# Later keys' activations made one group ahead and kept on chip, V alone for the first groups, and one norm for all gathered tokens

## The chip, the cores and the metric

The kernel runs on one core of one Trainium2 chip. The metric is the device time of one execution in microseconds (us); before takes 4829.66 us, the median of three runs (4826.51 to 4833.37).

## The reference, cut to what matters

The program is one layer on 512 tokens of width 2048: a mixer (mLSTM and forgetting attention), a cross attention, and a PEER feed-forward net, each followed by a layer norm. The change touches only the last of the three:

```python
def peer_ffn(x, w_pq, sub_keys, expert_u, expert_v):
    ...
    idx = jnp.take_along_axis(cand_i, best_pos, -1)
    g = jax.nn.softmax(best_s, -1)
    ...
    def block(args):
        xt, it, gt = args
        u = expert_u[it]
        a = jnp.einsum('tkd,td->tk', u, xt, preferred_element_type=F32)
        hact = jax.nn.gelu(a, approximate=False) * gt
        return jnp.einsum('tk,tkd->td', hact.astype(x.dtype), expert_v[it])
...
x = layer_norm(DN_ALPHA * x + h, ln_w[l, 2], ln_b[l, 2])
```

There are 16384 experts, 128 keys of 128. Each token takes 8 heads x 16 = 128 of them: a dot product with a row of `peer_u`, a gelu, a gate, and a sum of rows of `peer_v`. Everything is float32.

## The kernel before, in words

**Two ways for the tokens.** The 512 tokens stand in four blocks of 128. The first block's 128 tokens and 96 of the last block's, in two parts of 64 and 32, go the *gathered* way: their rows of `peer_u` and `peer_v` are fetched one by one (`gathered`, L906 to L955). The 288 tokens between (NDENSE) go the *dense* way: all 16384 experts are computed for them, and the gate matrix G, which is zero for experts that a token did not choose, picks the right ones.

**The dense way** has three parts, and most of the last 1760 us.

- `stage_a(c)` (L1269) computes for key c (128 experts) the product of `uT[c]` with the tokens: two weight tiles of 128 x 1024, 48 matmuls with 288 columns. Float32 accuracy is had by splitting each operand in a high and a low part: `split` (L132) makes the high part with a cast on ACT (whi, hph: L133) and the low part with a subtraction on DVE (wlo, hpl: L134), and `products` (L197) issues the three products (L201). A gelu on ACT (L1283) takes the result from PSUM to a tile `ga` (three buffers).
- `stage_h(c)` (L1304) multiplies the activation with key c's gates (L1313, DVE) and splits the product (hph on ACT, hpl on DVE). The split pairs have 18 buffers, for nine keys.
- `stage_o(c0, q)` (L1395) is V: for a group of eight keys (c0 to c0 + 7) and a quarter q of the 2048 output columns, four blocks of one weight tile and 24 matmuls each, summed in four PSUM banks (`po`) and then added to `acc` on DVE (L1422).

Weight tiles arrive through two rings, each with three raw buffers and two or three split ones. SP issues their loads (L145), in program order with all other loads of SP, so ACT and DVE can work about five tiles ahead of PE.

**Spilling.** Activations are computed well ahead of V. `ahead` gives for each key how many stage_a come before it: 76 (LOOK) before the first group, then the other 52 spread over the groups, three or four in a group, put behind V's blocks by `fill` (L1459). All but two of the 128 activations (`spilled`) are written to DRAM after their gelu (`gad`, L1285, issued by ACT) and read back by `fetch` (L1290 to L1302; L1299, issued by SP) up to two keys ahead of their stage_h into four buffers `gb`.

**The gate matrix** is built beside the first pass of stage_a, in 72 batches of four tokens (L1225 to L1255): two comparisons on DVE (L1244), four scalings on ACT (L1249), four matmuls (L1250), four copies on ACT (L1253). Every twelve batches, four DMAs on ACT's queue write the result to DRAM (`gd`, L1255). `fetch` reads it back four keys at a time (L1295, SP, two buffers `G`). The read waits for all the writes, since both name the whole of `gd`.

**The gathered way** runs beside all this: POOL fetches rows (L901), DVE makes dot products (L929) and sums (L932), paced by `fill`, 44 of 194 steps (EARLY) in the first pass (the first block is done before). At the end of each of the two parts, the rows' two or four partial sums are folded with matmuls (L950) and copied back by ACT (L951), and the part is normed by itself: two loads of the norm's weights, broadcast to all partitions (L964), statistics (L972), square root (`rstd`, L245), and four passes on DVE (`fin`, L976 to L983).

**The end.** After the last group `turned_out` (L1352) transposes `acc` back to rows, and `last_rows` (L1366) finishes the norm: square root, transpose of five columns of statistics (L1378), a copy (L1380), small matmuls (L1388), one DVE pass (L1390), output (L1393).

A static order of the instructions on each engine is fixed when the kernel is built: the source gives priorities, and a scheduler with its own estimates of durations puts each engine's instructions in a row. Engines run their row strictly in order.

Of the kernel before, what the change touches and what calls it, by code (L numbers as in the profile page):

```python
# [10 lines left out]
F32 = mybir.dt.float32  # L11
# [10 lines left out]
P = 128  # L22
# [23 lines left out]
def build(tc, I, out):  # L46
    nc = tc.nc
    with ExitStack() as ctx:
# [854 lines left out]
            after(i, last())  # L903
            return rows

        def gathered(t, r0, n, i, last, lag):  # L906


            ei, gg = eid[:, i], egg[:, i]
            xacc = gat.tile([P, D], F32, tag="xacc", bufs=1, name=nm("xacc"))  # L910
            for j in range(0, P, n):
                nc.gpsimd.dma_start(xacc[j:j + n], x2d[t, r0:r0 + n].rearrange("p g c -> p (g c)"))
            dots = gat.tile([P, P], F32, tag="dots", bufs=2, name=nm("dots"))
            held = []

            def use():
                s, rows = held.pop(0)
                k = s % n
                if s == n:

                    al = gat.tile([P, 1], F32, tag="al", bufs=1, name=nm("al"))
                    if n < P:
                        nc.vector.memset(al, 0.0)
                    nc.vector.memset(al[:n], ALPHA)
                    nc.scalar.mul(xacc, xacc, al)
                    nc.scalar.activation(dots[:, :n], dots[:, :n], AF.Gelu)
                    nc.vector.tensor_mul(dots[:, :n], dots[:, :n], gg[:, :n])
                if s < n:
                    after(nc.vector.scalar_tensor_tensor(rows, rows, 1.0, xacc, op0=ALU.mult, op1=ALU.mult,  # L929
                                                         accum_out=dots[:, k:k + 1]), last())  # L930
                else:
                    after(nc.vector.scalar_tensor_tensor(xacc, rows, dots[:, k:k + 1], xacc,  # L932
                                                         op0=ALU.mult, op1=ALU.add), last())

            for s in range(2 * n):
                if len(held) == lag:
                    use()
                held.append((s, gather_rows("peer_v" if s >= n else "peer_u", ei, s % n, last)))
                yield True
            while held:  # L940
                use()
            if n < P:
                fold = gat.tile([P, 64], F32, tag="fold", bufs=1, name=nm("fold"))
                nc.vector.tensor_add(fold[:, :n], ident[:, 0:n], ident[:, n:2 * n])
                for j in range(2 * n, P, n):
                    nc.vector.tensor_add(fold[:, :n], fold[:, :n], ident[:, j:j + n])
                for g in range(4):
                    bank = BK["pool"].tile([P, 512], F32, tag="s1", bufs=1, name=nm("fo"))
                    o = xacc[:, g * 512:(g + 1) * 512]
                    nc.tensor.matmul(bank[:n], fold[:, :n], o, start=True, stop=True)  # L950
                    nc.scalar.copy(o[:n], bank[:n])  # L951
            lw = fin_load(gat)
            fin_stats(i, xacc, range(4), n)
            fin(t * P + r0, i, xacc, lw, n)
            yield True  # L955
# [304 lines left out]
        mn = ctx.enter_context(tc.tile_pool(name="main", bufs=1, reuse_waits="tile"))  # L1260
        acc = mn.tile([P, NK, NDENSE], F32, tag="acc", name="acc")

        LOOK = 76
        EARLY = 44
        GA_N = 3
        J = 8
        gas, hs, gates = {}, {}, [None]

        rings[:] = [W, E]  # L1269

        def stage_a(c):

            bank = sm_bank()[:, :NDENSE]
            for kt in range(2):
# [7 lines left out]
            ga = gap.tile([P, NDENSE], F32, tag="ga", bufs=GA_N, name=nm("ga"))  # L1282
            nc.scalar.activation(ga, bank, AF.Gelu)  # L1283
            if c in spilled:
                nc.scalar.dma_start(gad[c], ga)  # L1285
            else:
                gas[c] = ga

        fetched = {}

        def fetch(c):

            if c % 4 == 0:
                gt = mn.tile([P, NDENSE // GB, 4, GB], F32, tag="G", bufs=2, name=nm("G"))
                nc.sync.dma_start(gt, gd[:, :, c:c + 4])  # L1295
                gates[0] = gt
            if c in spilled:
                ga = mn.tile([P, NDENSE], F32, tag="gb", bufs=4, name=nm("gb"))
                nc.sync.dma_start(ga, gad[c])  # L1299
            else:  # L1300
                ga = gas.pop(c)
            fetched[c] = ga, gates[0]  # L1302

        def stage_h(c):  # L1304
            for f in range(c, min(c + 3, NC_)):
                if f in fetched:
                    continue
                if f != c and f not in spilled:
                    break
                fetch(f)  # L1310
            ga, gt = fetched[c]
            gv = ga.rearrange("p (b t) -> p b t", t=GB)
            nc.vector.tensor_mul(gv, gv, gt[:, :, c % 4])  # L1313
            a, b = pair(mn, "hp", [P, NDENSE], 2 * J + 2)
            split(a, b, ga)
            hs[c] = (a, b)

        jobs = chain(*(gathered(TB - 1, r0, n, 1 + i, lambda: work["last"], 1) for i, (r0, n) in enumerate(GATHERED)))
        NT = -(-NDENSE // P)
        yw, last_norm = {}, {}  # L1320

        def columns_load():
# [12 lines left out]
            st = gp2.tile([P, NT, 32], F32, tag="st", name="st")  # L1335
            nc.vector.memset(st, 1.0)
            cs5 = gp2.tile([P, NT, 5], F32R, tag="cs5", name="cs5")
            nc.vector.tensor_copy(cs5[:, :, 0:2], st[:, :, 0:2])
            last_norm.update(w=w, rw=rw, st=st, cs5=cs5)
            for t in range(NT):  # L1340
                yw[t] = gp2.tile([P, D], F32, tag=f"yw{t}", name=f"yw{t}")

        def size(t):
            return min(P, NDENSE - t * P)

        def weighted(t, q, bank):
            n, sl = size(t), slice(q * 512, (q + 1) * 512)
# [16 lines left out]
                    rest.append(bank)  # L1364
            return rest

        def last_rows(rest):

            st, cs5, rw = last_norm["st"], last_norm["cs5"], last_norm["rw"]
# [4 lines left out]
            nc.vector.tensor_sub(cs5[:, :, 4], st[:, :, 27], cs5[:, :, 2].bitcast(F32))  # L1374
            tb = BK["pool"].tile([P, 512], F32, tag="s1", bufs=1, name=nm("t5"))
            for t in range(NT):
                n = size(t)
                nc.tensor.transpose(tb[:5, t * P:t * P + n], cs5[:n, t].bitcast(F32), ident[:n, :n])  # L1378
            l5 = gp2.tile([P, 512], F32R, tag="l5", name="l5")
            nc.scalar.copy(l5[:5, :NDENSE], tb[:5, :NDENSE])  # L1380
            for t in range(NT):
                weighted(t, 3, rest[t])
            for t in range(NT):
                n = size(t)
                for q in range(4):
                    sl = slice(q * 512, (q + 1) * 512)
                    bank = sm_bank()
                    nc.tensor.matmul(bank[:n], l5[:5, t * P:t * P + n], rw[:5, sl], start=True, stop=True)  # L1388
                    o = yw[t][:n, sl]
                    nc.vector.scalar_tensor_tensor(o, o, st[:n, t, 26:27], bank[:n], op0=ALU.mult, op1=ALU.add)  # L1390
                    if q % 2:
                        row, sl = (t + 1) * P, slice((q - 1) * 512, (q + 1) * 512)
                        (nc.sync, nc.scalar)[q // 2].dma_start(out[row:row + n, sl], yw[t][:n, sl])  # L1393

        def stage_o(c0, q, fill):  # L1395

# [2 lines left out]
            for m in range(J // 2):  # L1399
# [29 lines left out]
                nc.vector.scalar_tensor_tensor(acc[:, b], xt, ALPHA, acc[:, b], op0=ALU.mult, op1=ALU.add)  # L1429
            if last:  # L1430
                rest = turned_out(q)
                if q == 3:
                    last_rows(rest)


        ahead = [min(NC_, LOOK + -(-c * (NC_ - LOOK) // (NC_ - J))) for c in range(NC_)]
        spilled = {a for c in range(NC_) for a in range(ahead[c - 1] if c else 0, ahead[c]) if a - c >= GA_N - 1}
        njobs, done = sum(2 * n + 1 for _, n in GATHERED), 0
        for a in range(ahead[0]):
            stage_a(a)  # L1440
            while done * LOOK < a * EARLY:
                next(jobs, None)
                done += 1

        turn_g = [0]
# [88 lines left out]
```

## Time and profile before

| | before |
|---|---|
| median of three runs | 4829.66 us (4826.51 to 4833.37) |
| the profiled execution | 4827.06 us, its span 4825.3 us |
| granted TensorE clock, mean | 0.988 |
| PE busy | 4695.9 us, 97% |
| DVE / ACT / POOL busy | 77% / 46% / 19% |
| DMA | 1435.00 MB, mean 297 GB/s |
| first gelu of the first pass (L1283) | 3073.13 us |
| first V matmul | 3617.68 us |
| last gelu | 4735.7 us |

The span runs from the first to the last instruction; the execution's own time is 1.8 us longer. A share of busy time is a mean over stages that have different limits. All that the change touches lies behind 3066 us; there, 3066 to 3618 is the first pass (stage_a of the first 76 keys with the G build), and 3618 to 4805 are the 16 groups.

### The profile page before, as it was taken

To read this page: it belongs to the slowest core of one execution; us is meant where nothing else is said; L and a number is where in the kernel's file an instruction comes from. 1 tells how busy PE (TensorE), PEld (TensorE's weight loads), DVE (VectorE), ACT (ScalarE), POOL (GpSimd) and SP (SyncE) were. 2 spreads that over 40 slices of the span, in tenths; PEclk is the share of its full clock that TensorE was granted. 3 is DMA by queue.
4 is the path that set the end of the run, shared out by engine and by line. 5 is a ranking of instruction groups with operands and counts; after the bars stand their busy time and mean duration, and the time that the engine had idled before them with its cause. 6 is when DMAs were issued, how large, how long until landed. Compare 5 with 4: busy or idle time off the path is not lost. (4 is left out here: it accounts for less than half of the span.)

```text
span 4825.3 us, 75381 instructions
## 1 busy us (share of the span) xinstructions
PE 4695.9 (97%) x28720; PEld 4343.2 (90%) x28720; DVE 3736.9 (77%) x5326; ACT 2203.7 (46%) x3388; POOL 932.2 (19%) x884
## 2 busy tenths in 40 slices
PE   7999999999999899999989999999999999999999
PEld 6889788887888899999988779999999999999998
DVE  7776677766699777888769586899877888888886
ACT  6665666555543223343332334444874333343333
POOL 0000111200002332333334120111101222221110
PEclk9999999999999999999999999999999999999999
DMA  7888999865669899998889585588789999999993
GB/s 263 287 287 294 316 333 326 283 218 190 194 202 356 326 363 342 340 333 327 303 306 383 196 307 185 201 289 285 275 309 353 347 349 352 351 333 348 364 360 121
DMA packets 384380, 1435.00 MB, mean 297 GB/s; under 512 B 44412, under 2 KB 109676, under 8 KB 325392
## 3 DMA queue, kind: packets, MB, share of 16 engines
q1 hardware_dynamic: 268176, 832.52, 49.2%
q0 software_dynamic: 91456, 556.10, 30.8%
q10 hardware_dynamic: 24384, 41.56, 2.3%
q8 instruction: 225, 3.69, 0.3%
q14 instruction: 139, 1.14, 0.1%
HBM read 1338.10 MB, written 91.76 MB: 296 GB/s over the span
## 5 line engine op out<-in xcount | busy, mean ns | idle before, releaser
L134 DVE TENSOR_TENSOR wlo<-raw,whi 128x1024 fp32r<-128x1024 f32 x1472 | 1782.0, 1220 | 746.3 <-ACT whi L133 512.9
L133 ACT CAST whi<-raw 128x1024 fp32r<-128x1024 f32 x1472 | 1527.9, 1052 | 1710.7 <-PE mm L201 878.0
L201 PE MATMUL po<-hph,whi 128*128 128x288 f32 x2048 | 551.2, 296 | 9.9 <-ACT whi L133 9.9
L201 PE MATMUL sm<-Ch,whi 128*128 128x288 f32 x2048 | 557.8, 298 | 2.4 <-ACT whi L133 1.3
L201 PE MATMUL sm<-Cl,whi 128*128 128x288 f32 x2048 | 556.7, 296 | 0.0
L201 PE MATMUL po<-hpl,whi 128*128 128x288 f32 x2048 | 551.0, 296 | 0.5 <-DVE hpl L134 0.5
L901 POOL DMA_INDIRECT rows<-in_peer_u,eid x224 | 324.1, 1447 | 1173.5 <-DVE rows L929 486.8
L932 DVE SCALAR_TENSOR_TENSOR xacc<-rows,dots,xacc 128x2048 f32<-128x2048 f32 x224 | 525.4, 2345 | 21.6 <-DMA rows<-in_peer_v,eid 20.1
L901 POOL DMA_INDIRECT rows<-in_peer_v,eid x224 | 369.4, 1649 | 872.4 <-DVE xacc L932 464.4
L929 DVE SCALAR_TENSOR_TENSOR rows<-rows,xacc 128x2048 f32<-128x2048 f32 x224 | 511.3, 2285 | 24.1 <-DMA rows<-in_peer_u,eid 23.2
L201 PE MATMUL mm<-xh,whi 128*128 128x384 f32 x1280 | 437.7, 344 | 7.2 <-ACT whi L133 4.2
L201 PE MATMUL mm<-xl,whi 128*128 128x384 f32 x1280 | 430.9, 338 | 0.0
L201 PEld LDWEIGHTS po<-hph,whi 128*128 128x128 f32 x2048 | 383.9, 189 | 12.0 <-ACT whi L133 11.1
L201 PEld LDWEIGHTS sm<-Ch,whi 128*128 128x128 f32 x2048 | 384.9, 188 | 4.1 <-ACT whi L133 2.4
L201 PEld LDWEIGHTS po<-hpl,whi 128*128 128x128 f32 x2048 | 383.8, 189 | 2.4 <-issue 1.7
L201 PEld LDWEIGHTS sm<-Cl,whi 128*128 128x128 f32 x2048 | 385.0, 188 | 0.0
L201 PE MATMUL po<-hph,wlo 128*128 128x288 f32 x2048 | 337.9, 297 | 2.6 <-DVE wlo L134 2.5
L201 PE MATMUL sm<-Ch,wlo 128*128 128x288 f32 x2048 | 327.4, 298 | 1.1 <-DVE wlo L134 1.0
L201 PEld LDWEIGHTS po<-hph,wlo 128*128 128x128 f32 x2048 | 294.1, 189 | 7.1 <-DVE wlo L134 5.3
L201 PEld LDWEIGHTS sm<-Ch,wlo 128*128 128x128 f32 x2048 | 288.5, 188 | 3.8 <-DVE wlo L134 2.8
L201 PE MATMUL mm<-xh,wlo 128*128 128x384 f32 x1280 | 255.1, 335 | 0.0
L201 PEld LDWEIGHTS mm<-xh,whi 128*128 128x128 f32 x1280 | 242.2, 189 | 14.3 <-ACT whi L133 4.5
(440 smaller groups left out, 8527.7 us busy)
## 6 DMA issues: line engine op xcount, KB each, us to landing
raw<-in_w_in SPq DMA_DIRECT2D x512, 512.0 KB
raw<-in_uT SPq DMA_DIRECT2D x256, 512.0 KB
raw<-in_vq SPq DMA_DIRECT2D x256, 512.0 KB
raw<-in_w_xkv SPq DMA_DIRECT2D x64, 512.0 KB
raw<-in_w_br_ml SPq DMA_DIRECT2D x64, 512.0 KB
raw<-in_w_br_fx SPq DMA_DIRECT2D x64, 512.0 KB
raw<-in_w_out SPq DMA_DIRECT2D x64, 512.0 KB
raw<-in_peer_wq SPq DMA_DIRECT2D x64, 512.0 KB
```

The source lines that it names most:

```text
L133: nc.scalar.copy(hi, src)
L134: return nc.vector.tensor_sub(lo, src, hi.bitcast(F32))
L201: nc.tensor.matmul(o, w if stat else x, x if stat else w, start=k == first and x is xh and not part, stop=k == last and part == 1)
L901: i = nc.gpsimd.indirect_dma_start(out=rows, out_offset=None, in_=I[table], in_offset=bass.IndirectOffsetOnAxis(ap=ei[:, k:k + 1], axis=0))
L929: after(nc.vector.scalar_tensor_tensor(rows, rows, 1.0, xacc, op0=ALU.mult, op1=ALU.mult, accum_out=dots[:, k:k + 1]), last())
L932: after(nc.vector.scalar_tensor_tensor(xacc, rows, dots[:, k:k + 1], xacc, op0=ALU.mult, op1=ALU.add), last())
```

## The change

In the first pass stage_a runs for 72 keys instead of 76. Those 72 activations go to DRAM as before. The groups c0 = 0 to 56 then run V alone, without any stage_a. The groups c0 = 64 to 112 each run stage_a and stage_h for the eight keys of the next group between their own V blocks, one key behind every second block; these activations stay in the buffers `ga` and are never written to DRAM. The last group runs V alone. The gathers' pace is laid down anew: 46 of 194 steps in the first pass, then about 6 a group in V-only groups and 16 in groups with stage_a, done before the last two groups. stage_h reads gates and activations through `gates` and `fetched`, up to two keys ahead, as `fetch` did.

The two gathered parts of the last block no longer norm themselves. Each writes its sums to a DRAM tile `yg` (a DMA on POOL's queue); in the last group all 96 rows are loaded (`yw[NT]`), and after its second quarter `gathered_rows` norms them together in the way of `last_rows`.

In the changed kernel most lines named above stand one to four lower, the gate multiply ten higher (stage_a's gelu L1286, G batch L1248 to L1257, `gd` L1259, G read L1297, activation read L1300, multiply L1303).

```diff
@@ gathered
-        def gathered(t, r0, n, i, last, lag):
+        def gathered(t, r0, n, i, last, lag, keep=None):
...
+            if keep is not None:
+                nc.gpsimd.dma_start(keep, xacc[:n])
+                yield True
+                return
             lw = fin_load(gat)
@@ stage_a, stage_h
-        LOOK = 76
-        EARLY = 44
-        GA_N = 3
         J = 8
-        gas, hs, gates = {}, {}, [None]
+        LOOK = 72
+        EARLY = 46
+        fetched, hs, gates = {}, {}, {}
...
-            if c in spilled:
+            if c < LOOK:
                 nc.scalar.dma_start(gad[c], ga)
             else:
-                gas[c] = ga
+                fetched[c] = ga
...
         def stage_h(c):
+
             for f in range(c, min(c + 3, NC_)):
-                if f in fetched:
-                    continue
-                if f != c and f not in spilled:
-                    break
-                fetch(f)
-            ga, gt = fetched[c]
+                if f // 4 not in gates:
+                    gates[f // 4] = mn.tile([P, NDENSE // GB, 4, GB], F32, tag="G", bufs=2, name=nm("G"))
+                    nc.sync.dma_start(gates[f // 4], gd[:, :, f:f + 4])
+                if f < LOOK and f not in fetched:
+                    fetched[f] = mn.tile([P, NDENSE], F32, tag="gb", bufs=4, name=nm("gb"))
+                    nc.sync.dma_start(fetched[f], gad[f])
+            ga = fetched[c]
             gv = ga.rearrange("p (b t) -> p b t", t=GB)
-            nc.vector.tensor_mul(gv, gv, gt[:, :, c % 4])
+            nc.vector.tensor_mul(gv, gv, gates[c // 4][:, :, c % 4])
@@ the gathered tokens' norm
+        FIRST, NG = NDENSE % P, P - NDENSE % P
+        yg = dp.tile([NG, D], F32, tag="yg", name="yg")
+        jobs = chain(*(gathered(TB - 1, r0, n, 1 + i, lambda: work["last"], 1, yg[r0 - FIRST:r0 - FIRST + n])
+                       for i, (r0, n) in enumerate(GATHERED)))
...
+            yw[NT] = gat.tile([P, D], F32, tag="xacc", bufs=1, name="yw_g")
+            nc.gpsimd.dma_start(yw[NT][:NG], yg)
...
+        def gathered_rows():
+
+            st, y = last_norm["st"], yw[NT]
+            for q in range(4):
+                nc.vector.bn_stats(st[:NG, NT, 6 * q:6 * q + 6], y[:NG, q * 512:(q + 1) * 512])
+            nc.vector.bn_aggr(st[:NG, NT, 24:26], st[:NG, NT, 0:24])
+            for q in range(4):
+                weighted(NT, q, y[:, q * 512:(q + 1) * 512])
+            last_rows(NT, NT + 1, None)
@@ stage_o
-                if q == 3 and not last:
+                if q == 3 and c0 + J < LOOK:
...
                 rest = turned_out(q)
+                if q == 1:
+                    gathered_rows()
                 if q == 3:
-                    last_rows(rest)
+                    last_rows(0, NT, rest)
@@ the main loops
-        ahead = [min(NC_, LOOK + -(-c * (NC_ - LOOK) // (NC_ - J))) for c in range(NC_)]
-        spilled = {a for c in range(NC_) for a in range(ahead[c - 1] if c else 0, ahead[c]) if a - c >= GA_N - 1}
         njobs, done = sum(2 * n + 1 for _, n in GATHERED), 0
-        for a in range(ahead[0]):
+        for a in range(LOOK):
             stage_a(a)
...
+        room = [4 if c0 < LOOK - J else 10 for c0 in range(0, NC_ - 2 * J, J) for _ in range(2 * J)]
+        TOTAL, passed = sum(room), [0, 0]
         for c0 in range(0, NC_, J):
             def fill(i, c0=c0):
-                if i % 2:
-                    c = c0 + i // 2
-                    while turn_g[0] < njobs - EARLY and turn_g[0] * (NC_ - 16) <= c * (njobs - EARLY):
+                if i % 2 and LOOK <= c0 + J < NC_:
+                    a = c0 + J + i // 2
+                    stage_a(a)
+                    stage_h(a)
+                if room:
+                    passed[0] += room.pop(0)
+                    while passed[1] < njobs - EARLY and passed[1] * TOTAL <= passed[0] * (njobs - EARLY):
                         next(jobs, None)
-                        turn_g[0] += 1
-                    for a in range(ahead[c], ahead[c + 1] if c + 1 < NC_ else NC_):
-                        stage_a(a)
+                        passed[1] += 1
```

More of the change, by code (lines that the diff above doesn't have):

```diff
@@ L1334, in columns_load @@
                 nc.gpsimd.dma_start(rw[k:k + 1], t[j:j + 1])
-            st = gp2.tile([P, NT, 32], F32, tag="st", name="st")
+            st = gp2.tile([P, NT + 1, 32], F32, tag="st", name="st")
             nc.vector.memset(st, 1.0)
-            cs5 = gp2.tile([P, NT, 5], F32R, tag="cs5", name="cs5")
+            cs5 = gp2.tile([P, NT + 1, 5], F32R, tag="cs5", name="cs5")
             nc.vector.tensor_copy(cs5[:, :, 0:2], st[:, :, 0:2])
@@ L1365, in turned_out, with last_rows @@
             return rest
-        def last_rows(rest):
-            st, cs5, rw = last_norm["st"], last_norm["cs5"], last_norm["rw"]
+        def last_rows(t0, t1, rest):
+            rw, blocks = last_norm["rw"], range(t0, t1)
+            st, cs5 = last_norm["st"][:, t0:t1], last_norm["cs5"][:, t0:t1]
             rstd(st[:, :, 26], st[:, :, 25], (st[:, :, 28], st[:, :, 29]))
@@ L1375, in last_rows @@
             tb = BK["pool"].tile([P, 512], F32, tag="s1", bufs=1, name=nm("t5"))
[L1376 to L1384, printed above, removed]
+            for t in blocks:
+                n, o = size(t), (t - t0) * P
+                nc.tensor.transpose(tb[:5, o:o + n], cs5[:n, t - t0].bitcast(F32), ident[:n, :n])
+            l5 = gp2.tile([P, 512], F32R, tag="l5", name=nm("l5"))
+            m = sum(size(t) for t in blocks)
+            nc.scalar.copy(l5[:5, :m], tb[:5, :m])
+            for t in blocks:
+                if rest:
+                    weighted(t, 3, rest[t])
+            for t in blocks:
+                n, o = size(t), (t - t0) * P
+                row = (t + 1) * P if t < NT else S - NG
                 for q in range(4):
```

26 lines of the change are left out of this document (6 added, 20 removed).

## The prediction, made before the changed kernel ran

> **What bounds the kernel now.** I read the page first, then the stages by windows, then PE's waits in the last stage, and then single stretches.
>
> ```profile
> PE 4695.9 (97%) x28720; PEld 4343.2 (90%) x28720; DVE 3736.9 (77%) x5326; ACT 2203.7 (46%) x3388; POOL 932.2 (19%) x884
> L201 PE MATMUL po<-hph,whi 128*128 128x288 f32 x2048 | 551.2, 296 | 9.9 <-ACT whi L133 9.9
> ```
>
> ```profile
> core 0: us, PE busy (x) PEld busy (x) DVE busy (x) ACT busy (x) POOL busy (x), PEclk, DMA share, GB/s
> 3583.00:3618.00 35.00, 35.00 (x266) 35.00 (x265) 20.80 (x26) 13.29 (x20) 4.76 (x3) 1.00 1.02 385
> 3618.00:4800.00 1182.00, 1165.84 (x8655) 1151.36 (x8655) 966.55 (x1114) 448.16 (x568) 239.44 (x163) 1.00 0.89 333
> ```
>
> ```profile
> engine line waited for: us in total, times, longest us
> PE po L201 <- ACT whi L133: 9.9, 5, 2.0
> PE t L1378 <- DVE cs L1374: 5.6, 1, 5.6
> PE po L201 <- DVE wlo L134: 2.5, 9, 0.6
> PE sm L201 <- ACT whi L133: 1.3, 1, 1.3
> ```
>
> PE is the bound, and nearly full in the stage that the change rewrites: from the first V block (3618) to 4800 it idles 1182 - 1165.84 = 16.2 us. Everything that a better interleaving can win is in these 16 us and in what they do to the clock. Of them 9.9 us are five waits of a V matmul for its split weights, and 1.3 us is one of a stage_a matmul. The 5.6 us is in the tail, which the change leaves alone. The 35 us ahead of 3618 have no idle PE at all; I come back to them.
>
> One of the five waits, on ACT and then on PE:
>
> ```profile
> 3946.50 0.41 ACT L1283 ACTIVATE ga<-sm 128x288 f32<-128x288 f32 x1 [13.23 <-PE sm L201]
> 3946.95 0.33 ACTq L1285 DMA_DIRECT2D gad<-ga  x1
> 3947.37 3.89 ACT L133 CAST whi<-raw 128x1024 fp32r<-128x1024 f32 x4 [0.45 <-ACT ga L1283]
> ```
> ```profile
> 3945.24 1.23 PE L201 MATMUL sm<-Ch,wlo 128*128 128x288 f32 x8
> 3948.46 0.40 PE L201 MATMUL po<-hph,whi 128*128 128x288 f32 x1 [2.00 <-ACT whi L133]
> ```
>
> ACT had waited 13.2 us for PE to end a stage_a, because that key's gelu stands in ACT's queue ahead of four casts of weights. PE's next matmul needs the first of the casts. So gelu, DMA issue and cast lie on PE's path: 2.00 us.
>
> **What each such wait costs beyond its idle time.** The 9 us from each wait on:
>
> ```profile
> 3948.00:3957.00 9.00, 8.54 (x53) 8.54 (x53) 6.86 (x7) 5.35 (x6) 4.01 (x2) 0.81 0.80 266
> 4035.00:4044.00 9.00, 8.53 (x64) 8.53 (x65) 8.55 (x8) 5.26 (x6) 4.38 (x2) 1.00 0.94 322
> 4166.00:4175.00 9.00, 8.86 (x55) 8.86 (x56) 8.39 (x9) 5.02 (x6) 1.17 (x2) 0.81 0.90 313
> 4412.00:4421.00 9.00, 8.37 (x51) 8.37 (x52) 8.39 (x8) 5.53 (x6) 1.91 (x2) 0.81 1.00 399
> 4628.00:4637.00 9.00, 8.17 (x61) 8.17 (x62) 8.19 (x9) 5.73 (x6) 1.69 (x1) 1.00 0.98 382
> ```
>
> The time of one matmul comes from a full stretch of the first pass, 3250 to 3300:
>
> ```profile
> L201 PE MATMUL sm<-Ch,whi 128*128 128x288 f32 x125 | 33.7, 297 | 0.0
> L201 PE MATMUL sm<-Cl,whi 128*128 128x288 f32 x125 | 33.7, 293 | 0.0
> L201 PE MATMUL sm<-Ch,wlo 128*128 128x288 f32 x128 | 19.6, 295 | 0.0
> ```
>
> 378 in 50 us are 0.132 us each, so a key's stage_a (48 matmuls) takes 6.35 us and a V block (24) 3.2 us. The busy time of the five windows would hold 64, 64, 67, 63 and 62 matmuls; they hold 53, 64, 55, 51 and 61. Three of five waits also cost some 12 matmuls, 1.5 us, in a window with a granted clock of 0.81: about 4.8 us in all. *The Trainium skill, "TensorE: Matmul & The Clock Gate", section "HAM oscillation — how this bites in real kernels", has it that only idle gaps of more than about 3.4 us bring the clock down. By that rule these 2 us gaps would cost their idle time alone and the sum below would be some 5 us higher; the trace disagrees in three cases of five, and I go by the trace.*
>
> **The change part by part.**
>
> *The five waits: gone.* I compared the order of ACT's and PE's instructions in the two builds. Before has exactly five gelus whose next cast is needed one matmul after the stage_a that the gelu waits for; after has none, its shortest lead is 3 us, and where stage_a and V alternate (7 groups) casts run 10 us or more ahead of PE. That is -9.9 and -4.8. The 1.3 us wait at 4492 stood behind the 2.0 us scaling of a gathered part's sum (L925) on ACT; after the reorder that has room too: -1.3. **Together -16.0.**
>
> *The start of V: later.* V's first matmul needs key 0's gated activation, whose gates (G) are read back from DRAM. That read (L1295, on SP) waits for the last write of the gate table (L1255), hence for all 72 batches of the G build. In before PE's order has 271 matmuls of the first pass, the last 5.6 keys, between the last G batch and the first V matmul. In after it has none: the first pass is four keys shorter and has two more gather jobs of DVE ahead of G. PE's order goes: end of the last key, the last eight G batches, V. So what those 36 us (the window 3583 to 3618, full) hid now lies open. Step by step from rows of before:
>
> ```profile
> 3363.90 0.38 PE L201 MATMUL sm<-Ch,whi 128*128 128x288 f32 x1
> 3364.11 0.61 PE L1250 MATMUL po<-o,o 128*128 128x128 f32 x4
> 3364.48 0.38 PE L201 MATMUL sm<-Cl,whi 128*128 128x288 f32 x1
> ```
> ```profile
> 3575.44 1.28 ACT L1249 ACTIVATE o<-o,gT 128x128 f32<-128x128 f32 x4 [0.40 <-DVE o L1244]
> 3576.63 0.74 ACT L1253 COPY stage<-po 128x128 f32<-128x128 f32 x4
> 3577.25 1.06 ACT L133 CAST whi<-raw 128x1024 fp32r<-128x1024 f32 x1
> 3582.18 0.33 ACTq L1255 DMA_DIRECT2D gd<-stage  x1
> 3582.55 5.01 ACTq L1255 DMA_DIRECT2D gd<-stage  x3
> ```
> ```profile
> 3594.83 0.61 SPq L1295 DMA_DIRECT2D G<-gd  x1
> 3605.32 0.82 DVE L1313 TENSOR_TENSOR ga<-ga,G 128x288 f32<-128x288 f32 x2
> 3605.80 0.81 ACT L133 CAST hph<-ga 128x288 fp32r<-128x288 f32 x2 [0.69 <-DVE ga L1313]
> 3617.68 0.30 PE L201 MATMUL po<-hph,whi 128*128 128x288 f32 x1
> ```
> ```profile
> q10 hardware_dynamic: 1008, 3.59, 37.9%
> ```
>
> - For PE, a batch is two runs of four records of 0.37 us and a slower neighbour, 0.9 us. Without any wait V would begin four keys earlier, at 3617.7 - 4 x 6.35 = 3592.3, and eight batches (7.3 us) before that the last key ends: T0 = 3585.0.
> - Eight batches on ACT from T0: scales 3575.44 to 3576.63 and copies to 3577.25 are 1.81 us a batch, 14.5 us. The last gelu (0.41) goes in, and the last copies (about 0.4) overlap the first write: 14.5.
> - Write of the table: first issue 3582.18 to the read's issue 3594.83 is 12.65 us, beside the raw loads of the pass. From 3582 to 3607 ACT's queue took 37.9% of 25 us of all engines, 9.5 us, 0.8 of it two activations: 8.7 is the floor. After T0 the weight rings are full and the queues emptier: I take 11.
> - Read of G until the gate multiply: 3594.83 to 3605.32 is 10.5 us, beside a second G, four activations and raw loads. By bytes (0.58 of 3.59 MB) it is 1.5 us; half the row, 5.3, is my floor. I take 8.
> - Multiply and cast: 0.45 and 0.43.
>
> Sum: 34.4 us (30 to 38.5), of which 7.3 are PE's own batches: PE stands **27 us (22 to 31)**. *The Trainium skill, "DMA: Bandwidth & Descriptors", section "Anatomy of one DMA", gives a fixed 2.0 us a transfer, most of it the receipt from the target memory; with that on top of the bytes the write takes 10.7 and the read 3.5, and PE would stand 22 us.*
>
> After it the clock has to come back: a 2 us gap cost 0 to 1.5 us, so I take **2** (0 to 4). In the first group each activation buffer (four) and G buffer (two) is filled only after its last use, on SP in this order; before had 12 us of room here (3605.8 to 3617.7), now none: **1** (0 to 3). Together +30.
>
> *V alone (8 groups of 51 us), then V with stage_a (7 of 102).* The matmuls are the same. The DMA share stays at the 0.89 of the window or little above in the first kind, and some 16 MB of activations no longer go through DRAM. In the second kind a kept activation waits for its pair of split buffers until the fourth quarter of its group, and the gelu three keys on waits for that on ACT; the casts behind are needed 10 us later: **0** (0 to 3 a group).
>
> *The gathered parts.* The removed norms (their loads, Sqrt and Gelu tables, four passes each) lie on DVE, ACT, POOL and SP beside a full PE: 0. New on PE's path are two things:
>
> ```profile
> L950 PE MATMUL fo<-xacc,fold x16: 592/604/643, 4228.6 to 4709.4; 128*64 128x512 f32 x8, 128*32 128x512 f32 x8
> L951 ACT COPY xacc<-fo x8: 575/578/582, 4229.7 to 4710.0; 64x512 f32<-64x512 f32 x4, 32x512 f32<-32x512 f32 x4
> 4812.23 0.73 PE L1378 MATMUL t<-ident,cs 128*5 128x128 f32 x3 [5.63 <-DVE cs L1374]
> 4813.44 3.74 PE L1388 MATMUL sm<-rw,l 5*128 5x512 f32 x6 [0.48 <-ACT l L1380]
> ```
>
> In the second fold three of the four matmuls now stand nearly in a row, and each needs the bank that ACT's copy of the last one frees (0.60 + 0.58): **+1.5** (0 to 2.5). The norm of the 96 gathered rows inside the last group puts a transpose, a copy and four matmuls between V matmuls: as in the tail, 0.5 us of idle and 0.7 a matmul less what DVE has ready: **+1.8** (0 to 3.5).
>
> **Sum:** -16.0 + 30 + 1.5 + 1.8 = **+17.3 us**. The profiled execution took 4827.06 (span 4825.3), 2.6 under the median of 4829.66; +17.3 on the one is 4844.4, on the other 4847.0. I predict **4846**.
>
> **Rivals.**
> - **A, faster: the start of V is hidden.** Where the eight G batches reach ACT before T0, since ACT and DVE run ahead of PE there, and write and read go at the bytes' pace, PE would hardly stand, and the saved 16 us decide: 4829.7 - 16 + 3.3 = 4817 with no stand at all. It is faster by more than a measurement can miss from a stand under 3 us. Against it: the eight batches' results come from PE matmuls that stand behind the last key, and the bytes alone take 10 us. Chance 0.12.
> - **B, half of it.** The copies follow PE at 0.9 us a batch instead of 1.81 (scales done early), write and read at their floors: 7.3 + 8.7 + 5.3 + 0.9 = 22, less 7.3: a stand of 15. 4829.7 - 16 + 15 + 6 = 4835, about the same. Chance 0.13.
> - **C, slower still: a new wait takes the place of the old five.** If the kept activations (three buffers) hold up ACT in the seven alternating groups by what one of the five waits cost, 2.0 + 1.0 us each, that is +21: 4867. For it: a gelu then waits on DVE, which is 82% busy in the window. Against: casts lie 10 us ahead. Chance 0.08.
> - **D, the change doesn't do what it says:** the waits stay, because what makes them is a stage_a's end ahead of a cast, and seven groups still alternate: 4846 + 14.7 = 4861. Chance 0.04.
>
> **How the numbers follow.** The forecast has 0.63. 0.2% of this kernel, 9.7 us, is about what a measurement tells from no change. Slower by more than that (above 4839.3): C, D and nine tenths of the forecast's own 0.63, with a little of B: 0.71. Faster by more (below 4820): most of A: 0.10. The rest, 0.19, lies within. The range runs from just above A to the lower edge of C: 4825 to 4862; the forecast's own is 4836 to 4858.
>
> **What would show it.** In the profile after: a single PE wait of 22 to 31 us ahead of the first V matmul, for a cast of ACT (hph), with SP waiting for the table's writes; the first V matmul near 3619 although the first pass ends four keys earlier; the five waits for whi gone from the list; PE idle between V's start and the last group below 6 us. The forecast is wrong if PE has other work ahead of V, if the G chain takes under 15 us, or if waits of several us stand in each alternating group.

## The result, and the profile after

The changed kernel takes **4840.15 us** (median of 12 runs, 4832.18 to 4851.75), the kernel before 4828.43 (12 runs, 4825.77 to 4833.37): a ratio of **1.0027**, with a 95% interval of 1.0018 to 1.0035. So it is some 13 us slower, 9 to 17. Run again later, unaltered and beside other runs of before, it gave 1.0035 (1.0022 to 1.0047). The forecast was 4846, in a range of 4825 to 4862.

The profiled execution took 4839.53 us (span 4837.8). The waits of PE from the first pass to the end, as in the list of before (what waited, for what: total, times, longest):

```profile
PE po L201 <- ACT hph L133: 15.7, 1, 15.7
PE t L1374 <- DVE cs L1370: 5.6, 1, 5.6
PE po L1254 <- ACT o L1253: 3.9, 7, 1.0
PE po L1254 <- DVE o L1248: 3.8, 1, 3.8
PE po L201 <- DVE hpl L134: 1.6, 1, 1.6
PE fo L950 <- ACT xacc L951: 0.9, 2, 0.7
PE sm L1387 <- ACT l L1377: 0.9, 2, 0.5
```

The five waits for whi are gone, and so is the one of stage_a. In their place stand one of 15.7 us, for the first cast of an activation, and eight on batches of the G build, 7.7 us, of which 6 us lie behind the last key. So nearly all of it is in one place, the passage from the first pass to V. It is read from the four engines in turn:

```profile
3589.28 2.29 DVE L929 SCALAR_TENSOR_TENSOR rows<-rows,xacc 128x2048 f32<-128x2048 f32 x1 [3.52 <-DMA rows<-in_peer_u,eid]
3591.50 0.69 DVE L1248 TENSOR_TENSOR o<-iota,i0T 128x512 f32<-128x512 f32 x1
...
3621.85 1.20 DVE L1303 TENSOR_TENSOR gb<-gb,G 128x288 f32<-128x288 f32 x3 [17.01 <-DMA gb<-gad]
```
```profile
3592.28 1.28 ACT L1253 ACTIVATE o<-o,gT 128x128 f32<-128x128 f32 x4 [3.08 <-DVE o L1248]
...
3607.50 0.33 ACTq L1259 DMA_DIRECT2D gd<-stage  x1
...
3622.35 1.17 ACT L133 CAST hph<-gb 128x288 fp32r<-128x288 f32 x3 [14.37 <-DVE gb L1303]
```
```profile
3616.59 0.61 SPq L1297 DMA_DIRECT2D G<-gd  x1
```
```profile
3592.94 1.16 PE L1254 MATMUL po<-o,o 128*128 128x128 f32 x8 [3.84 <-DVE o L1248]
...
3605.81 1.36 PE L1254 MATMUL po<-o,o 128*128 128x128 f32 x8 [0.47 <-ACT o L1253]
3622.83 0.61 PE L201 MATMUL po<-hph,whi 128*128 128x288 f32 x1 [15.67 <-ACT hph L133]
```

PE's last key ends 3.84 us ahead of 3592.94, at 3589.1. From there to V it is the chain of the forecast: the last G batches on ACT until the first write at 3607.50, the write until SP may issue the read at 3616.59, the read until the gate multiply at 3621.85, and multiply and cast until 3622.83. What the forecast did not have is the first DVE line: a gather product waits 3.52 us for its rows, and the comparisons of a G batch stand behind it.

From V on the time is less than before, and PE is fuller:

```profile
core 0: us, PE busy (x) PEld busy (x) DVE busy (x) ACT busy (x) POOL busy (x), PEclk, DMA share, GB/s
3618.00:4800.00 1182.00, 1173.56 (x8761) 1162.89 (x8762) 960.54 (x1104) 459.60 (x578) 211.68 (x159) 1.00 0.86 318
```

This window still holds 5 us of the long wait; before it had 1165.84 us of PE and 8655 matmuls. The pace went from 134.7 to 134.0 ns a matmul (busy time over count); part of that is the granted clock, which three of the five waits had brought down.

**How the account is split.** The first gelu of the first pass starts at 3073.1 us in the trace of before and at 3076.7 in that of after (groups of tile ga). The order of all engines up to the first pass is the same in the two builds, and in the eleven runs below that time lies between 3068.9 and 3083.6. So what lies ahead of it is the variation of executions, and I count from it, in two parts: the **passage** (first gelu to first V matmul, less 6.35 us for each key of the first pass) and the **groups** (first V matmul to the end of the span, less 6.35 us for each key that is left).

| trace | keys first | first gelu | first V matmul | span | passage | groups |
|---|---|---|---|---|---|---|
| before | 76 | 3073.1 | 3617.7 | 4825.3 | 62.0 | 877.4 |
| after | 72 | 3076.7 | 3622.8 | 4837.8 | 88.9 | 859.4 |
| after, run again | 72 | 3080.1 | 3623.7 | 4842.2 | 86.4 | 862.9 |

The passage costs 24.4 to 26.9 us more, the groups 14.5 to 18.0 us less. The net is 8.9 and 9.9 us in these traces, and 13 by the ratio of the runs (the medians lie 11.7 and 14.7 us above those of before). A trace of a build whose engines have the order of before up to the first fold (before with one norm, below) has a passage of 66.7; against that one the passage costs 19.7 to 22.2 us.

### The profile page after: what moved, and what is told of

Read it like the earlier page. It is cut to its first block, busy times and chain, and to the rows that moved or that the text cites. A ratio compares the mean times of both kernels' runs of the same rounds, so it can differ in the third digit from the quotient of the medians.

```text
span 4837.8 us, 75281 instructions
## 1 busy us (share of the span) xinstructions
PE 4696.1 (97%) x28725; PEld 4345.1 (90%) x28725; DVE 3737.3 (77%) x5319; ACT 2208.4 (46%) x3384; POOL 903.1 (19%) x883
## 5 line engine op out<-in xcount | busy, mean ns | idle before, releaser
L201 PE MATMUL po<-hph,whi 128*128 128x288 f32 x2048 | 545.5, 296 | 15.7 <-ACT hph L133 15.7
L901 POOL DMA_INDIRECT rows<-in_peer_v,eid x224 | 345.1, 1541 | 911.7 <-DVE wlo L134 444.9
L201 PEld LDWEIGHTS po<-hph,whi 128*128 128x128 f32 x2048 | 380.5, 189 | 18.7 <-ACT hph L133 16.1
```

What stands on the lines that cost most here:

```text
L201: nc.tensor.matmul(o, w if stat else x, x if stat else w, start=k == first and x is xh and not part, stop=k == last and part == 1)
L901: i = nc.gpsimd.indirect_dma_start(out=rows, out_offset=None, in_=I[table], in_offset=bass.IndirectOffsetOnAxis(ap=ei[:, k:k + 1], axis=0))
```

## The experiments

The main theory: the way of the gate table through DRAM stands open ahead of V, since the shorter first pass leaves PE nothing to do meanwhile; and the interleaving by whole groups does what it was to do, it removes the waits. Rivals: the loss lies in the groups; the wait moves along whatever the length of the pass; the one norm is what costs. Each experiment ran in 5 rounds beside the kernel before on one chip; the column "before" is the median on that chip.

| run | median us | before | ratio, interval | passage | groups |
|---|---|---|---|---|---|
| 80 keys first | 4829.64 | 4830.69 | 0.9993 (0.9985 to 1.0002) | 59.4 | 875.1 |
| gate table in four tiles | 4838.91 | 4830.69 | 1.0020 (1.0011 to 1.0029) | 87.9 | 860.1 |
| before with 72 keys | 4842.88 | 4830.69 | 1.0022 (1.0013 to 1.0031) | 85.4 | 870.3 |
| after with two norms | 4837.54 | 4830.69 | 1.0010 (1.0001 to 1.0018) | 87.6 | 861.3 |
| four tiles, buffers moved | 4834.32 | 4830.89 | 1.0003 (0.9994 to 1.0012) | 85.4 | 860.5 |
| 30 gather steps first | 4848.49 | 4830.89 | 1.0034 (1.0022 to 1.0046) | 59.5 | 899.2 |
| 80 keys, 50 steps, pace 3 | 4834.29 | 4830.89 | 1.0007 (0.9998 to 1.0016) | 58.7 | 885.7 |
| before with one norm | 4841.30 | 4830.89 | 1.0018 (1.0009 to 1.0026) | 66.7 | 886.1 |
| 80 keys, 52 steps | 4824.77 | 4828.08 | 0.9995 (0.9985 to 1.0004) | 59.9 | 873.3 |
| the same, two norms | 4822.37 | 4828.08 | 0.9989 (0.9980 to 0.9998) | 59.7 | 867.7 |

Passage and groups come from one profiled execution each. The same build differs by 2.5 and 3.5 us between two of them (after, above), and the same order of instructions by 4.7 us in the passage (before and before with one norm). The profiled execution can lie far from the median: 8.2 us above it with 30 gather steps first, 11.6 us below it in the last run. The medians are the better measure of a total, the traces of a place.

### More work ahead of V: 80 keys first

```diff
-        LOOK = 72
+        LOOK = 80
```

> The changed kernel with 80 keys ahead instead of 72. Theory (the G build's way through DRAM stands open ahead of V): PE's order now has 426 matmuls of the first pass (56 us) between the last G batch and V, so the 15.7 us wait ahead of the first V matmul and the 6 us of waits among the last G batches go, some 22 to 27 us: about 4815, and faster than the kernel before by 10 to 16 us, since the five waits stay away. Rival 1 (the time is lost in the groups, by V alone or by stage_a and V alternating): about 4840 still. Rival 2 (the wait moves with the end of the first pass, whatever its length): about 4840, with a wait of 15 us ahead of V.

The passage falls by 29.5 us against after, below that of before; no PE wait is left in it. That rejects the second rival: the wait is a matter of what PE has to do while the table is away. The total is not the first rival's 4840 either (4829.64). But it is that of before, not 10 us less. The groups took 875.1, 15.7 more than in after. Its waits beside the one in the tail:

```profile
PE po L201 <- ACT hph L133: 5.4, 3, 2.9
PE po L201 <- DVE wlo L134: 4.2, 5, 1.5
PE po L201 <- DVE hpl L134: 1.8, 1, 1.8
```

These are new, and all but one of them lie in the V-only groups (3760 to 4031). The longest, on DVE:

```profile
3912.70 2.36 DVE L134 TENSOR_TENSOR wlo<-raw,whi 128x1024 fp32r<-128x1024 f32 x2 [1.38 <-ACT whi L133]
3914.97 2.35 DVE L932 SCALAR_TENSOR_TENSOR xacc<-rows,dots,xacc 128x2048 f32<-128x2048 f32 x1
3917.24 1.19 DVE L1303 TENSOR_TENSOR gb<-gb,G 128x288 f32<-128x288 f32 x3
```

The gate multiplies of the next group stand in DVE's row behind a gather sum of 2.35 us, the cast hph waits for them, and PE for the cast. From V to the tail PE's waits come to 13.0 us, against 3.7 in after; and three of them are followed by 3.4 us at a granted clock of 0.50 (from 3814.0, 3919.8 and 3974.4), 1.7 us lost each. What was expected of this run left out both.

### Less cover in the kernel before: 72 keys instead of 76

```diff
-        LOOK = 76
+        LOOK = 72
```

> The kernel before with 72 keys ahead instead of 76, nothing else. PE's order then has 91 matmuls (12 us) of the first pass behind the last G batch instead of 271 (36 us). Theory: the chain from the last G batch to V takes about 25 to 30 us beside the pass, so PE stands 13 to 18 us ahead of V, and the time is 4840 to 4847. Rival (not the length of the pass but the reordered groups make the loss): within 3 us of before, 4828.

Measured: 12.5 us ahead of V (13 to 18 expected), a passage 23.4 us longer, and 1.0022 of before. So four keys fewer make nearly the whole loss of the passage without any other part of the change (18.7 us of it against the passage of 66.7). Its list of waits keeps those for whi (5.4 us in 3) and adds 8.8 us for wlo. This kernel holds the loss of the change and less than half of its gain: its groups took 870.3, 7 us less than in before and 7 to 11 more than in the changed kernel.

### What the read of the gates waits for

```diff
-        gd = dp.tile([P, NDENSE // GB, NC_, GB], F32, tag="gd", name="gd")
+        gd = [dp.tile([P, NDENSE // GB, 32, GB], F32, tag=f"gd{i}", name=f"gd{i}") for i in range(4)]
...
-                nc.scalar.dma_start(gd[:, hb, ch * 32:ch * 32 + 32], stage[ch])
+                nc.scalar.dma_start(gd[ch][:, hb], stage[ch])
...
-                    nc.sync.dma_start(gates[f // 4], gd[:, :, f:f + 4])
+                    nc.sync.dma_start(gates[f // 4], gd[f // 32][:, :, f % 32:f % 32 + 4])
```

> The changed kernel with the gate table in four DRAM tiles, one for each quarter of the keys, so that the first read of gates waits for one of the four last writes and not for all. Theory (the read waits for the whole table): the first read starts some 6 us sooner (0.77 of 3.1 MB to write), and the wait ahead of V falls from 15.7 to about 10 us: about 4834. Rival (the wait is for the activations or for the cast queue): no change, 4840.

The wait ahead of V stayed at 15.2 us: a miss. SP issued the read 9.1 us after the first write (3603.61 to 3612.70), as in after (3607.50 to 3616.59). In the compiled order the read still has the writes' semaphores among its waits, by another way: the gate buffer lies on memory of the G build's stage tiles, which the writes read. The trace does not tell the two ways apart. The next run moves the buffer, by laying out the split pairs ahead of it:

```diff
         acc = mn.tile([P, NK, NDENSE], F32, tag="acc", name="acc")
+        pair(mn, "hp", [P, NDENSE], 18)
```

> As the run with four DRAM tiles (which kept the wait at 15.2 us), and with the split pairs laid out ahead of the gate and activation buffers, so that the first gate buffer no longer lies on memory of the G build's stage tiles. In the compiled order the first read of gates then waits for the writes of one tile and for PE and DVE alone. Theory (the read waited for all four writes by two ways, the table and its own buffer's memory): the read starts about 3 us behind the first write instead of 9, the wait ahead of V falls to 9 or 10 us, and the time to about 4834. Rival (the four writes share the 16 engines and end together, so that one tile is no earlier than four): the wait stays at 15 us, 4839.

Its ACT, SP and DVE:

```profile
3605.13 0.33 ACTq L1259 DMA_DIRECT2D gd<-stage  x1
```
```profile
3608.44 0.61 SPq L1298 DMA_DIRECT2D G<-gd  x1
```
```profile
3617.39 1.20 DVE L1304 TENSOR_TENSOR gb<-gb,G 128x288 f32<-128x288 f32 x3 [14.92 <-DMA gb<-gad]
```

The read starts 3.3 us after the first write, as the theory had it. But it takes 8.95 us until the multiply, where after took 5.26 (3616.59 to 3621.85): it now shares the DMA engines with the three other writes (their busy share is 1.02 from 3608.4 to 3617.4, against 0.72 in after from 3616.6 to 3621.9). Of 5.8 us won at the start 3.7 are given back, and the wait is 13.6 us, not 9 or 10. So the theory was right on what the read waits for, and the rival right on what the writes and the read have in common. The ratio of 1.0003 is better than these 2 us explain; the traces differ by no more, and the rest stays open.

### Fewer gathers in the first pass

```diff
-        EARLY = 46
+        EARLY = 30
```

> The changed kernel with 30 instead of 46 gather steps in the first pass (118 more instead of 148 spread over the groups becomes 164). PE's order then has 378 matmuls (50 us) between the last G batch and V. Theory: the wait ahead of V and those among the last G batches go, -22 us, as in the run with 80 keys; the V-only groups carry 7.1 gather steps each (6.4 in the changed kernel, 6.9 in the run with 80 keys, which had some 11 us of new waits in them). If those waits come from DVE's load with gathers, about 4828 again with 10 us or more of waits in the V-only groups; rival (they came from that build's order alone): 4818 or less, with under 4 us of waits.

No wait ahead of V, as expected: with fewer gather products on DVE the G build ends 378 matmuls ahead of V. But the groups took 899.2, 40 us more than in after. Of its waits:

```profile
PE po L201 <- DVE wlo L134: 6.8, 3, 3.3
PE po L201 <- ACT hph L133: 6.5, 4, 2.5
PE fo L950 <- DVE xacc L932: 6.2, 1, 6.2
PE po L201 <- DVE acc L1431: 3.0, 2, 2.6
```

Three of the four are waits for DVE itself. In the V-only groups the waits come to 11 us, as the theory had it. The gathers that were moved out of the first pass come back as DVE's load in the groups, and at the fold PE waits 6.2 us for the last gather sum. The granted clock adds to it: it stood at 0.50 for 3.4 or 6.8 us after each of six waits and for 17 us around that fold; that is some 15 us more lost than in after. Waits (27 us against 4) and clock together are nearly the 40 us. The total, 4848.49, is above both the theory (4828) and the rival (4818), which counted neither the fold nor the clock.

### Fewer gathers in the V-only groups

```diff
-        LOOK = 72
-        EARLY = 46
+        LOOK = 80
+        EARLY = 50
...
-        room = [4 if c0 < LOOK - J else 10 for ...]
+        room = [3 if c0 < LOOK - J else 10 for ...]
```

> 80 keys ahead, 50 gather steps in the first pass, and a pace of 3 instead of 4 in V-only groups: 5.6 gather steps in each of them (6.9 in the run with 80 keys alone), 18.7 in the groups with stage_a. PE's order has about 34 us of the first pass behind the last G batch. Theory (the waits in V-only groups come from gather work ahead of the gate multiply on DVE): they fall to under 4 us, no wait ahead of V, and the time is 4816 to 4822, 8 to 14 us under the kernel before. Rival (waits move to the groups with stage_a, whose DVE is then fuller): 4828.

The waits for hph and wlo fell to 2.8 and 1.0 us, as the theory said; but the groups with stage_a then carry 18.7 gather steps each, and the fold waited:

```profile
PE fo L950 <- DVE xacc L932: 14.0, 1, 14.0
PE po L201 <- ACT hph L133: 2.8, 1, 2.8
```

The total, 4834.29, lies above the theory (4816 to 4822) and above the rival's 4828 too: the waits did move to the groups with stage_a, as the rival had it, but to the fold, which it did not name. With 80 keys ahead there are six groups with stage_a instead of seven, and what is taken from the V-only groups is too much for them.

### The load of the changed kernel, with cover

```diff
-        LOOK = 72
-        EARLY = 46
+        LOOK = 80
+        EARLY = 52
```

The changed kernel was run once more beside it:

> The changed kernel once more, unaltered, on the same chip as the next two runs. By the first result it is 1.0027 of the kernel before (1.0018 to 1.0035), so 4839 to 4848 here, with a wait of 13 to 18 us ahead of V in the trace.

It came out at 4842.73, with a wait of 15.1 us.

> 80 keys ahead and 52 gather steps in the first pass, so that the V-only groups carry 6.6 gather steps each and the others 16.5, nearly the 6.4 and 16.1 of the changed kernel (the run with 80 keys alone had 6.9). PE's order has 32 us of the first pass behind the last G batch, which the chain to V of about 25 us fits in. Theory 1 (the new waits of the run with 80 keys come from the gather load and the place of the gathers in DVE's row): from the first V matmul on the time is as in the changed kernel, so the wait ahead of V is gone at no cost: 4815 to 4820. Theory 2 (a build without a stand ahead of V has no lead in its weight rings and pays in the V-only groups whatever the load): 10 us or more of waits there, 4828 to 4832.

4824.77: 18 us less than the changed kernel on the same chip, and 0.9995 of before. It lies between the two theories. From its list:

```profile
PE po L201 <- ACT hph L133: 5.8, 2, 5.3
PE fo L950 <- DVE xacc L932: 3.5, 1, 3.5
PE po L201 <- DVE hpl L134: 3.3, 3, 2.5
```

The 5.3 us are in the first group, at 3657. There the second four activations are read when the first four leave their buffers, as the forecast had it:

```profile
3645.68 3.95 SPq L1300 DMA_DIRECT2D gb<-gad  x3
```
```profile
3651.27 2.28 DVE L929 SCALAR_TENSOR_TENSOR rows<-rows,xacc 128x2048 f32<-128x2048 f32 x1
3653.48 0.08 DVE L929 DVE_READ_ACCUMULATOR rows<-rows,xacc 128x1 f32 x1
3653.48 2.29 DVE L929 SCALAR_TENSOR_TENSOR rows<-rows,xacc 128x2048 f32<-128x2048 f32 x1
3655.70 0.08 DVE L929 DVE_READ_ACCUMULATOR rows<-rows,xacc 128x1 f32 x1
3655.97 0.46 DVE L1303 TENSOR_TENSOR gb<-gb,G 128x288 f32<-128x288 f32 x1 [0.20 <-DMA gb<-gad]
```

Issued from 3645.68 on, they land near 3656, with the DMA engines full (share 1.04), and two gather products stand ahead of the multiply. In after the same reads went out at a share of 0.60 (3623.4 to 3631.8). So a stand ahead of V pays for something: the first group's reads. The other V-only groups have 4.7 us of waits (of 0.4 us and more) against 1.6 in after. With the first group's that is over 10 us, the amount that theory 2 named; about half of it has another cause than theory 2's weight rings, and the total is below its 4828, so the run decides against neither theory outright.

### The one norm

> The changed kernel with the old two norms of the gathered parts (undoes that part of the change alone). The forecast put +3.3 us on the one norm and the second fold; the trace of the changed kernel shows only 0.9 and 0.9 us of waits there. Theory: 0 to 2 us faster than the changed kernel, 4838 to 4840. Rival (the two removed norms were a good part of the saving in the groups): 5 us or more slower than the changed kernel, 4845 or more.

> The kernel before with the one norm of all gathered tokens, nothing else of the change. The forecast put +3.3 us on it with the second fold; the changed kernel's trace shows 1.8 us of waits at its instructions, and the run without it is 2.6 us faster than the changed kernel. Theory: 0 to +3 us against the kernel before. Rival (the removed norms had held ACT and DVE in front of casts): 3 us or more faster than before.

> The last one with the old two norms of the gathered parts. The one norm on the kernel before took about 9 us more (3 us of matmuls and transposes on PE, 6 us of waits in a reordered DVE and ACT). Theory: 3 to 8 us faster than the last one. Rival (there is no cost to the one norm where V runs alone): within 2 us of it.

The edit takes away, or in the second run adds alone, `keep`, `yg` and `gathered_rows`. On the kernel before, the one norm costs: 1.0018 (1.0009 to 1.0026), 4 to 13 us, more than the theory (0 to 3) and against the rival. All engines' orders are the same up to the first fold; from there to the end of the span before takes 596.7 us (4228.6 to 4825.3) and this build 606.3 (4240.6 to 4846.9). The list of waits from V on has more for wlo than that of before:

```profile
PE po L201 <- ACT whi L133: 11.3, 6, 2.0
PE sm L201 <- DVE wlo L134: 6.5, 6, 2.5
PE po L201 <- DVE wlo L134: 3.4, 13, 0.6
```

So it is the order behind the fold that changed, at places that have nothing to do with the norm. In the changed kernel the traces show no difference: with two norms the groups took 861.3, against 859.4 and 862.9 in after, and the passage is that of after. The medians do: with two norms 6.9 us above the kernel before of the same chip, with one 11.7 and 14.7. So 0 to 8 us of the changed kernel's loss may be the one norm's, and the third rival is not excluded as a part of it. With 80 keys and 52 steps it is 2.4 us by the medians, between theory (3 to 8) and rival (within 2), and the two intervals overlap. All three comparisons point to the same side; the size in the changed kernel stays open, and it is not the two norms' removal that saved time in the groups.

The last of these runs, 80 keys, 52 steps and two norms, is faster than both kernels: 4822.37, 0.9989 of before (0.9980 to 0.9998), which is just clear of no change.

## Why the prediction was right, by its steps

- **The five waits: gone.** As forecast, with the wait at 4492. Idle PE from V to the tail fell from 15.9 to 3.7 us (6.3 in the second trace of after, which has a new wait of 2.9 us for wlo). The 4.8 us of clock in the sum were right: three stretches of 3.4 us at a granted clock of 0.50 in before, 5.1 us lost, and none in after once the clock is back from the stand (one in the second trace).
- **The start of V: later.** 26.9 us (24.4 in the second trace) against 27. By terms: the G batches from the last key's end to the first write 18.4 us against 14.5; write 9.1 against 11 (floor 8.7); read 5.3 against 8 (floor 5.3); multiply and cast 1.0 against 0.9. Sum 33.7 against 34.4. Two errors cancelled, and that the total fits so well is luck. The first term was too small by 3.9 us, the DVE stall behind a gather; write and read went near their floors, since the queues were as empty as the forecast said, and it should have taken its own floors there. That half of rival B came true; its other half, copies at PE's pace, did not. *The forecast's estimate by the Trainium skill, "DMA: Bandwidth & Descriptors", section "Anatomy of one DMA", was 10.7 us for the write and 3.5 for the read; the section is written for transfers that GpSimd (POOL) issues, and ACT and SP issue these.*
- **What the stand looks like.** Not one wait of 22 to 31 us, but 15.7 and, among the last batches, 6 us: the forecast's own arithmetic had ACT at 1.81 us a batch against PE's 0.9, and so waits between them. PE idled 21.6 us of those 33.7, a little under the forecast's 22 to 31, and was busy for 12.1 with the eight batches, which were put at 7.3.
- **The clock after it**: 2 us in the sum. In the first 9 us, 49 matmuls where 68 fit, at a mean granted clock of 0.70 (0.50 for the first 5.5 us, then 1.00):

```profile
3622.80:3631.80 9.00, 8.97 (x49) 8.97 (x50) 5.21 (x14) 4.33 (x10) 0.00 (x0) 0.70 0.62 176
```

  19 x 0.132 = 2.5 us. *The Trainium skill, "TensorE: Matmul & The Clock Gate", section "HAM oscillation — how this bites in real kernels", asks for a gap of more than 3.4 us; this one of 15.7 us agrees, the three 2 us gaps of before do not.*
- **The first group**: 1 us in the sum; 0.4 us of waits in after and 2.9 in its second trace, both for wlo and none for the reads; 5.3 us in a build where V starts without a stand.
- **Second fold and the norm's matmuls**: +3.3 in the sum; 0.9 and 0.3 us of waits ahead of the tail, and 4 matmuls of 0.4 us.
- **The sum.** +17.3 forecast, 13 (9 to 17) measured. What was mis-sized lies in the groups: forecast -9.7 from V on (-16.0 + 2 + 1 + 1.5 + 1.8), measured -18.0 and -14.5. The traces show 12.2 and 9.6 us of idle PE less, and 2.4 and 1.2 us less lost to the clock; the forecast left the small waits for wlo standing (2.5 us in before; 0.4 and 2.9 in after), and about 3.5 us of the gain are not accounted for by waits or clock.
- **The cause.** The forecast put the missing cover down to the four keys fewer and to the two more gather steps. The first is shown from both sides: before with 72 keys has a passage of 85.4, and 80 keys in the changed kernel take it to 59.4. Gather steps in the first pass act too: 30 instead of 46 take it to 59.5. What the two more steps do by themselves is not shown: before with 72 keys has 44 steps, and its 85.4 lies only 1.0 to 3.5 us under after, less than traces of one order differ.

## What to carry to other kernels

When work is moved from one side of a hand-over to the other, look for what it was covering: here four keys of stage_a hid the last batches of a table, its write and its read back, and their 20 to 27 us cost more than the 14 to 18 us that the removal of five waits and what went with it brought. A wait that is taken away by adding cover does not give its whole length back: the traffic and the DVE work that the stand let through unhindered must then be done beside a full PE; here that was 5.3 us for the first group's reads alone. And a dependency can have two ways (a table, and the memory of a buffer); what is gained by cutting both is bounded by the engines that both transfers share.

## What the runs showed of the hardware that was not expected

Three of the five idle gaps of 1.9 to 2.0 us in before brought the granted clock down to 0.50 for 3.4 us (0.81 is the mean over 9 us), and two did not. The three drops start at 3949.0, 4167.4 and 4413.2, which is 64 and 72 times 3.413 us apart, as if the clock were set anew in steps of that length. The trace in such steps, at the first gap and at the one that ends at 4035.5 (columns as above):

```profile
3945.60:3949.00 3.40, 1.40 (x11) 1.17 (x10) 0.56 (x1) 2.04 (x3) 0.00 (x0) 1.00 0.78 263
3949.00:3952.40 3.40, 3.40 (x16) 3.40 (x16) 3.40 (x3) 2.34 (x4) 1.32 (x1) 0.50 0.69 253
4030.90:4034.30 3.40, 2.58 (x20) 2.34 (x18) 3.13 (x2) 0.41 (x1) 2.35 (x1) 1.00 0.37 139
4034.30:4037.70 3.40, 2.23 (x16) 2.23 (x17) 2.25 (x2) 3.32 (x4) 0.59 (x1) 1.00 0.71 207
4037.70:4041.10 3.40, 3.40 (x28) 3.40 (x27) 3.40 (x5) 1.53 (x3) 2.81 (x1) 1.00 0.99 377
```

The first gap lies within one step (PE busy for 1.40 of 3.40 us), and the next step has half the clock. The second falls across two steps (busy 2.58 and 2.23), and nothing follows. The other two that cost the clock lie like the first (busy 1.46 and 1.40), the fifth like the second (2.08 and 2.77). So what a gap cost here hung on where it fell. The bound is not shown: in the run with 80 keys a step with PE busy for 1.90 us was followed by half the clock, and one with 1.65 was not.

Counted from the first write, a read that started 5.8 us sooner, while three other writes of 0.77 MB each were under way, ended only 2.1 us sooner. And builds whose engines have the same order up to the first pass start it between 3068.9 and 3083.6 us, and the passages of two builds with the same order up to the first fold differ by 4.7 us, so one profile a build cannot place a difference of 5 us.
